# A decoder block with expert retrieval: 576 instead of 640 tokens on the dense path, its down product transposed, and one gathered tile's dot products moved into the front

## The chip, the cores and the metric

One core of a Trainium2 chip runs the whole block in one launch. The metric is the device time of one execution in microseconds (us). Engines: TensorE (PE, its weight loads PEld), VectorE (DVE), ScalarE (ACT), GpSimd (POOL), SyncE (SP, which issues most DMAs); 16 DMA engines move the data.

## The reference, cut to what matters

1024 tokens of 1024 channels. The mixing sub-layer (norm, one input projection, a gated convolution beside sliding-window attention, an output projection) is followed by expert retrieval: per token 8 heads, two key halves, the best 16 of 128 each, the best 16 sums; so 128 of 16384 experts, each with a row u and a row v.

```python
def peer_ffn(h, wq, keys, u_tab, v_tab):
    def chunk(ht):
        q = (ht @ wq).reshape(t, PEER_HEADS, 2, PEER_DK)
        sa = jnp.einsum('thd,hnd->thn', q[:, :, 0], keys[0])
        sb = jnp.einsum('thd,hnd->thn', q[:, :, 1], keys[1])
        va, ia = lax.top_k(sa, PEER_TOPK)
        vb, ib = lax.top_k(sb, PEER_TOPK)
        ...
        top, pos = lax.top_k(cand, PEER_TOPK)
        eidx = jnp.take_along_axis(cidx, pos, axis=-1)
        g = jax.nn.softmax(top, axis=-1)
        u = u_tab[eidx]
        v = v_tab[eidx]
        a = jax.nn.gelu(jnp.einsum('thkd,td->thk', u, ht))
        return jnp.einsum('thk,thkd->td', g * a, v)
```

The result is multiplied by a gate of the conditioning and added to the residual.

## The kernel before

The front works on three groups of tokens, 384, 384 and 256, with channels on the partitions (`front`, L307). A group runs 18 input projections, convolution and attention, 8 output projections, the second norm, then 16 query projections (`proj`, L235), each 24 matmuls with the group's tokens as columns; every weight is split into a high part (ScalarE, L243) and a remainder (GpSimd, L244), and high x high, high x low and low x high are summed. `keys` and `top16` find the best keys on VectorE. The rest of the selection, `finish_topk` (L540, `select` L565), is a background task that runs beside the next group: `bg(us)` (L202) is called between projections and gives each task credit at its rate, one step per unit.

The expert sum is made in two ways. Tokens 0 to 639 go the dense way: `spread` (L655) turns a token's 128 picks into a 128 x 128 matrix of coefficients, from one-hot columns `oi` (made on ScalarE, GpSimd and VectorE by the pattern HOT, L673 to L679) and partners `oj` (L683), multiplied on TensorE (L686), four tokens a step, and stores it in `gd`. The dense stage (`dense`, L750) then runs over all 128 first key indices j, each with 128 experts: `up` (L779) multiplies a row of u with h2 for all dense tokens, `weigh1` and `weigh2` (L803, L811) apply gelu and the coefficients and split the result, and `down` (L835) multiplies with v once per four j, the weights stationary and 512 channels of v moving, for 5 token blocks and 2 channel halves; `flush` (L855) adds the product to an accumulator on VectorE. All splits of u, v and the weights are threefold products as above.

Tokens 640 to 1023 go the gathered way, three tiles of 128 tokens (`gather`, L691): for each of 128 picks one indirect DMA issued from GpSimd (L713) fetches a row of u (4 KB) for each of 128 tokens into a ring of six slots, and VectorE makes a dot product (L732, the tokens' h2 copied to PSUM); then the same for v, added up in PSUM (L740). So 768 gathers of 512 KB in 774 units, all spread over the dense stage at RATE 0.49 units per credited us (`bg` in L775 and L838).

The order on an engine is laid down at build time from the program's order and readiness: fetches of the first gathered tile stand among the third group's weight splits at 953 us.

## Time and profile before

| | us |
|---|---|
| median of 3 runs | 2877.46 |
| lowest and highest | 2875.39, 2883.49 |
| span of the profiled execution | 2871.6 |
| its own time around the span | not given by the page |
| first group, front | 0 to about 360 |
| second group | about 360 to 740 |
| third group | about 740 to 1045 |
| last selections and first ups | 1045 to 1160 |
| dense and gathered stage | 1160 to 2872 |

Busy times are sums over instructions of one engine; the span is from the first to the last instruction. An idle time stands ahead of the instruction that ended it, with what released it. DMA share is the mean busy share of the 16 DMA engines; with two queues on one engine it can pass 1.

### The profile page before, as it was taken

How to read it: one execution, taken by the hardware profiler on the slowest of the kernel's cores; microseconds unless marked ns; L12 is line 12 of the kernel's file. 1: busy time of each engine (PE TensorE's matmuls, PEld its weight loads, DVE VectorE, ACT ScalarE, POOL GpSimd, SP SyncE). 2: the span in 40 equal slices, each digit the busy share in tenths (PEclk: the TensorE clock that was granted, in tenths of full speed). 3: DMA queues.
4: the chain of work that ended last, by engine and by line, in shares of the span. 5: the costliest groups of instructions: out<-in, count | busy, mean ns of one | idle time of the engine just before them, and what ended most of it. 6: DMA issues, size and time to landing. Idle time of an engine off the chain costs nothing.

```text
span 2871.6 us, 44952 instructions
## 1 busy us (share of the span) xinstructions
PE 2710.1 (94%) x15567; PEld 2441.8 (85%) x15567; DVE 2391.0 (83%) x4853; ACT 1095.5 (38%) x2193; POOL 1727.9 (60%) x1491
## 2 busy tenths in 40 slices
PE   5999989899888889999999999999999999999998
PEld 3888978788687779889999898999999889989997
DVE  5665899878799778888888898888988888888886
ACT  2455467775476633322222232222223222222221
POOL 3534476665676745666666666666666666656661
PEclk7999989999899989999999999999999999999999
DMA  6647423355334576999999999999999999999995
GB/s 224 230 145 232 123 85 129 139 199 181 99 145 138 203 234 202 347 333 348 331 320 346 348 348 333 348 323 334 337 349 323 324 349 333 331 331 342 331 334 185
DMA packets 345032, 763.69 MB, mean 266 GB/s; under 512 B 31418, under 2 KB 130138, under 8 KB 341860
## 3 DMA queue, kind: packets, MB, share of 16 engines
q0 software_dynamic: 112320, 408.99, 39.2%
q1 hardware_dynamic: 231044, 349.21, 36.4%
q8 instruction: 122, 2.00, 0.3%
q10 hardware_dynamic: 1440, 2.62, 0.2%
q14 instruction: 106, 0.87, 0.1%
HBM read 701.45 MB, written 59.24 MB: 265 GB/s over the span
## 4 chain that ended last, share of the span: by engine, by line
PE 44%; DMA 8%; DVE 6%; issue 4%; POOL 2%; ACT 1%; SPq 0%; DVEq 0%; POOLq 0%; ACTq 0%
PE pv L845 23%; PE pa L788 21%; DMA vraw<-in_v 4%; DMA uraw<-in_uT 2%; DVE pq L740 1%; DVE vdL L832 1%; DVE rows L732 1%; DMA wraw<-in_wq 1%; DVE wdL L815 1%; DVE dacc L864 1%; ACT vdH L831 1%; POOL rows L713 1%; DVE more L732 1%; POOL uL L772 0%; DVE gw L807 0%
## 5 line engine op out<-in xcount | busy, mean ns | idle before, releaser
L788 PE MATMUL pa<-h,uH 128*128 128x320 f32 x4096 | 772.0, 310 | 14.5 <-ACT uH L771 6.3
L788 PEld LDWEIGHTS pa<-h,uH 128*128 128x128 f32 x4096 | 648.2, 189 | 22.0 <-ACT uH L771 7.3
L244 POOL TENSOR_TENSOR wL<-wraw,wH 128x512 fp32r<-128x512 f32 x252 | 360.7, 1440 | 263.2 <-ACT wH L243 224.8
L845 PE MATMUL pv<-vdH,wdH 128*128 128x512 f32 x1275 | 500.2, 392 | 14.7 <-DVE dacc L864 14.5
L845 PE MATMUL pv<-vdL,wdH 128*128 128x512 f32 x1275 | 498.1, 391 | 0.1
L845 PE MATMUL pv<-vdH,wdL 128*128 128x512 f32 x1275 | 497.1, 390 | 0.0
L788 PE MATMUL pa<-h,uL 128*128 128x320 f32 x2048 | 468.9, 310 | 2.9 <-POOL uL L772 2.9
L772 POOL TENSOR_TENSOR uL<-uraw,uH 128x512 fp32r<-128x512 f32 x256 | 343.6, 1343 | 149.5 <-ACT uH L771 140.3
L713 POOL DMA_INDIRECT rows<-in_u,eidx x257 | 259.1, 1008 | 164.7 <-DVE aw L732 100.0
L713 POOL DMA_INDIRECT rows<-in_v,eidx x254 | 252.5, 994 | 160.9 <-DVE pq L740 115.6
L788 PEld LDWEIGHTS pa<-h,uL 128*128 128x128 f32 x2048 | 344.0, 189 | 3.8 <-POOL uL L772 3.8
L740 DVE SCALAR_TENSOR_TENSOR pq<-rows,aw,pq 128x1024 f32<-128x1024 f32 x253 | 324.7, 1284 | 5.0 <-DMA rows<-in_v,eidx 2.5
L864 DVE TENSOR_TENSOR dacc<-dacc,pv 128x512 f32<-128x512 f32 x310 | 212.2, 685 | 137.5 <-PE pv L845 136.7
L831 ACT CAST vdH<-vraw 128x512 fp32r<-128x512 f32 x255 | 152.7, 619 | 437.1 <-DMA vraw<-in_v 386.2
L732 DVE CUSTOM_DVE_ANT_0 rows<-rows,pq 128x1024 f32<-128x1024 f32 x257 | 307.8, 1214 | 10.5 <-DMA rows<-in_u,eidx 10.1
L771 ACT CAST uH<-uraw 128x512 fp32r<-128x512 f32 x256 | 158.4, 620 | 384.1 <-DMA uraw<-in_uT 374.1
L845 PEld LDWEIGHTS pv<-vdH,wdH 128*128 128x128 f32 x1275 | 240.0, 188 | 70.9 <-DVE dacc L864 23.1
L845 PEld LDWEIGHTS pv<-vdH,wdL 128*128 128x128 f32 x1275 | 240.0, 188 | 50.6
L845 PEld LDWEIGHTS pv<-vdL,wdH 128*128 128x128 f32 x1275 | 240.1, 188 | 47.6 <-DVE vdL L832 0.5
L678 POOL TENSOR_SCALAR oi<-iota,tr 128x128 f32<-128x128 f32 x160 | 198.5, 1242 | 109.8 <-PE gps L686 89.4
L832 DVE TENSOR_TENSOR vdL<-vraw,vdH 128x512 fp32r<-128x512 f32 x255 | 193.7, 776 | 74.1 <-ACT vdH L831 73.6
L814 ACT CAST wdH<-gw 128x640 fp32r<-128x640 f32 x128 | 93.1, 728 | 402.6 <-DVE gw L807 393.7
(251 smaller groups left out, 5118.7 us busy)
## 6 DMA issues: line engine op xcount, KB each, us to landing
uraw<-in_uT SPq DMA_DIRECT2D x256, 256.0 KB, 6.3
vraw<-in_v SPq DMA_DIRECT2D x255, 256.0 KB, 6.0
gd<-stage SPq DMA_DIRECT2D x20, 2048.0 KB, 7.5
gt<-gd SPq DMA_DIRECT2D x160, 256.0 KB, 10.2
wraw<-in_w_in SPq DMA_DIRECT2D x108, 256.0 KB, 2.8
wraw<-in_wq SPq DMA_DIRECT2D x96, 256.0 KB, 2.8
wt<-in_w_ada SPq DMA_DIRECT2D x40, 512.0 KB, 4.7
wraw<-in_w_out SPq DMA_DIRECT2D x48, 256.0 KB, 2.7
```

The lines of the kernel that those rows point to most:

```text
L244: G.tensor_tensor(wL, w, wH.bitcast(F32), op=ALU.subtract)
L678: (G if who == "P" else V).tensor_scalar(oi, iota, tr[:, 0, t:t + 1], tr[:, 2, t:t + 1], op0=ALU.is_equal, op1=ALU.mult)
L713: G.indirect_dma_start(out=r, out_offset=None, in_=table, in_offset=bass.IndirectOffsetOnAxis(ap=eidx[:, ti, k:k + 1], axis=0))
L732: V.tensor_tensor_reduce(out=r, in0=r, in1=h2, op0=ALU.mult, op1=ALU.add, scale=1.0, scalar=0.0, accum_out=aw[:, k:k + 1])
L740: V.scalar_tensor_tensor(acc, r, aw[:, k:k + 1], acc, op0=ALU.mult, op1=ALU.add)
L771: A.copy(uH, raw)
L772: G.tensor_tensor(uL, raw, uH.bitcast(F32), op=ALU.subtract)
L788: PE.matmul(AT[j][:, s, 0:n], l[:, c, :], h2[r][4 * h + c][:, s * n:s * n + n], start=(h == 0 and c == 0 and k == 0), stop=(h == 1 and c = ...
L831: A.copy(vH, raw)
L832: V.tensor_tensor(vL, raw, vH.bitcast(F32), op=ALU.subtract)
L845: PE.matmul(pt, l[:, P * tt:P * tt + P], r, start=(m == 0), stop=(m == 3 * J - 1))
L864: V.tensor_tensor(dst, dst, pt, op=ALU.add)
```

## The change

The dense tokens become 128 to 703, 576 of them, and the gathered ones 0 to 127, 704 to 767 and 768 to 1023: four tiles of 128, 64, 128 and 128 tokens. The tile of 64 lies twice on the partitions, each copy with 64 of the 128 picks, so it takes 64 fetches of u and 64 of v: 896 gathers in all. The plan of the gathered work is a list GPLAN; its first 129 units (the held h2 rows and the 128 dot products of the first tile) run as a background task in the second and third group at 0.5 units per credited us, on three slots of a new ring of four rows that lives through both stages, with h2 held in the fourth; what isn't done is drained before the dense stage. The other 779 units run in the dense stage at 0.50 on eight slots. In the dense stage both products take 288 tokens as columns (two halves): in `down` a 128 x 128 piece of v is stationary and the weights move, so the output is transposed and goes to a second output `outT`, and the gate becomes a scalar per partition, one VectorE instruction for two. A row of u comes as one DMA of 512 KB (pieces of 4 KB) for two of 256. Three PSUM buffers of one bank for `up` and three for `down`, in place of two of two banks and two. HOT gives ScalarE 3 of 8 columns, GpSimd 2, VectorE 3. The residual's rows go to memory in row form only for gathered blocks, else as they lie. Front buffers are trimmed (`oi` 6 to 4, `tr` 2 to 1, `va`, `iu` 5 to 4, `sc` 4 to 3, x 4 to 3, the two norm buffers, a selection tile halved).

```diff
-DT0, DT = 0, 640
-G0 = 640
-GT = 3
+DT0, DT = 128, 576
+HN = DT // 2
+GTILES = [(0, 128), (704, 64), (768, 128), (896, 128)]
+GOFF = np.concatenate([[0], np.cumsum([w for _, w in GTILES])]).tolist()
+GT = len(GTILES)
+NG = GOFF[-1]
+OUTS = {"out": (NG, D), "outT": (P, NC, DT)}
 J = 4
 TB = 32
-HOT = "APVV"
-RATE0, RATE = 0.0, 0.49
+HOT = "APVAVAPV"
+RATEA, RATE = 0.5, 0.5
 ORDER = True
 BACK = 0
 ADA_RATE, ADA0 = 0.3, 0.0
@@ -61,8 +65,13 @@
 FIRST, SECOND = 8, 10
 CY, ROWS, EARLY = 0, 1, 0
 TM = 384
+GPLAN = []
+for _gi, (_, _w) in enumerate(GTILES):
+    GPLAN += [("h", _gi, 0)] + [("u", _gi, k) for k in range(_w)]
+    GPLAN += [("v", _gi, k) for k in range(_w)] + [("g", _gi, 0), ("x", _gi, 0)]
+NA = 129
 RING = 6
-XB = 4
+XB = 3
...
+    rowring = gat.tile([P, 4, D], F32, name="ring")
...
-                nc.sync.dma_start(dst[r0 + P * b:r0 + P * b + P, 512 * h:512 * h + 512], xt)
-
-        for b in range(nb):
-            to_rows(x2d, t0, b, [x2T], ident)
+                nc.sync.dma_start(dst[r0:r0 + P - skip, 512 * h:512 * h + 512], xt[skip:P, :])
+
+        dcols, dat = slice(d0 - t0, d1 - t0), slice(d0 - DT0, d1 - DT0)
+        for b, gi in gblocks.items():
+            g0, w = GTILES[gi]
+            to_rows(x2d, GOFF[gi], P - w, b, [x2T], ident)
+        if d1 > d0:
+            for h in range(2):
+                nc.sync.dma_start(x2t[:, 4 * h:4 * h + 4, dat], x2T[h][:, :, dcols])
         if ROWS:
             modulate2()
-        for b in range(nb):
-            if b >= nd:
-                to_rows(h2d, t0 - G0, b, [h2H, h2L], identr)
-        if nd:
+        for b, gi in gblocks.items():
+            to_rows(h2d, GOFF[gi], P - GTILES[gi][1], b, [h2H, h2L], identr)
+        if d1 > d0:
             for k in range(2):
-                for c in range(NC):
-                    src = ch(h2[k], c)[:, 0:P * nd].bitcast(F32)
-                    at = slice(t0 - DT0, t0 - DT0 + P * nd)
-                    nc.sync.dma_start(h2s[k, :, c, at], src)
+                for h in range(2):
+                    nc.sync.dma_start(h2s[k, :, 4 * h:4 * h + 4, dat], h2[k][h][:, :, dcols].bitcast(F32))
...
-        va = [lv.tile([P, 2 * PH, 16], F32, name="va", bufs=5) for b in range(nb)]
-        iu = [lv.tile([P, 2 * PH, 16], U32, name="iu", bufs=5) for b in range(nb)]
+        va = [lv.tile([P, 2 * PH, 16], F32, name="va", bufs=4) for b in range(nb)]
+        iu = [lv.tile([P, 2 * PH, 16], U32, name="iu", bufs=4) for b in range(nb)]
...
-            for b in (range(nb) if ORDER else [*range(nd, nb), *range(nd)]):
+            for s0, b in blocks:
                 r = yield from select(va[b], iu[b])
-                if b < nd:
-                    yield from spread(t0 // P + b, *r)
-                else:
-                    place((t0 - G0) // P + b, *r)
-                    placed.append(b)
-                    if len(placed) == 1:
-                        gtask.append(add(gather(), RATE0))
+                lo, hi = max(s0, DT0), min(s0 + P, DT0 + DT)
+                if hi > lo:
+                    yield from spread(s0, lo - s0, hi - s0, *r)
+                if b in gblocks:
+                    place(gblocks[b], *r)
+                    placed.append(gblocks[b])
...
+            r3, s3 = [t.rearrange("p (h k) -> p h k", h=PH) for t in (r, src)]
+            for h0 in range(0, PH, 4):
+                hs = slice(h0, h0 + 4)
+                hot1 = sel.tile([P, 4, 16, 16], BF16, name="hot1")
+                V.tensor_tensor(hot1, s3[:, hs].unsqueeze(2).to_broadcast([P, 4, 16, 16]),
+                                rank.unsqueeze(1).to_broadcast([P, 4, 16, 16]), op=ALU.is_equal)
+                V.tensor_tensor(hot1, hot1, id4[:, hs, s, :].unsqueeze(3).to_broadcast([P, 4, 16, 16]), op=ALU.mult)
+                m = 8
+                while m > 1:
+                    V.tensor_tensor(hot1[:, :, 0:m, :], hot1[:, :, 0:m, :], hot1[:, :, m:2 * m, :], op=ALU.add)
+                    m //= 2
+                V.tensor_tensor(r3[:, hs], hot1[:, :, 0, :], hot1[:, :, 1, :], op=ALU.add)
+                yield
...
-        for q in range(P // TB):
+        for q in range(p0 // TB, p1 // TB):
...
-                    oi = gb.tile([P, P], F32, name="oi", bufs=6)
+                    oi = gb.tile([P, P], F32, name="oi", bufs=4)
...
+    def gather(plan, slots, held=None):
+
         state = {"n": 0}
-        rows = gat.tile([P, 4, D], F32, name="rows", tag="stage"), gat.tile([P, RING - 4, D], F32, name="more")
 
         def row():
-            n = state["n"] % RING
+            n = state["n"] % len(slots)
             state["n"] += 1
-            return rows[n // 4][:, n % 4, :]
-
-        def fetch(u):
-            ti, n = divmod(u, 2 * P + 2)
+            return slots[n]
+
+        def rows_of(r, src, gi, whole=True):
+            w = GTILES[gi][1]
+            part = src[GOFF[gi]:GOFF[gi] + w, :]
+            G.dma_start(r[P - w:P, :], part)
+            if w < P and whole:
+                G.dma_start(r[0:w, :], part)
+
+        def fetch(unit):
+            kind, gi, k = unit
             r = row()
-            if n == 2 * P:
+            if kind == "h":
+                rows_of(r, h2d, gi)
+            elif kind == "g":
                 G.dma_start(r, g2d)
-            elif n > 2 * P:
-                G.dma_start(r, x2d[G0 + P * ti:G0 + P * ti + P, :])
+            elif kind == "x":
+                rows_of(r, x2d, gi, whole=False)
             else:
-                if n == 0:
-                    state["hr"] = row()
...
+        ring, at = [], 0
+        for kind, gi, k in plan:
+            while gi not in placed:
                 yield
-            ti, n = divmod(u, 2 * P + 2)
-            if n == 0:
-                aw = state["aw"]
-                h2 = state["hr"]
-                if "pq" in env:
-                    h2 = env["pq"].tile([P, D], F32, name="pq")
-                    A.copy(h2, state["hr"])
+            while at < len(plan) and len(ring) < len(slots) - 1 and plan[at][1] in placed:
+                ring.append(fetch(plan[at]))
+                at += 1
             r = ring.pop(0)
-            k = n % P
-            if n < P:
+            w = GTILES[gi][1]
+            if kind == "h":
+                h2 = held if held is not None else env["pq"].tile([P, D], F32, name="pq")
+                A.copy(h2, r)
+                aws[gi] = gat.tile([P, P], F32, name="aw", bufs=2)
+            elif kind == "u":
                 V.tensor_tensor_reduce(out=r, in0=r, in1=h2, op0=ALU.mult, op1=ALU.add, scale=1.0,
-                                       scalar=0.0, accum_out=aw[:, k:k + 1])
-            elif n == P:
+                                       scalar=0.0, accum_out=aws[gi][:, k:k + 1])
...
-        pa = es.enter_context(tc.tile_pool(name="pa", bufs=2, space=PSUM, side="right", reuse_waits="tile"))
+        pa = es.enter_context(tc.tile_pool(name="pa", bufs=3, space=PSUM, side="right", reuse_waits="tile"))
...
-                    raw = da.tile([P, 4, P], F32, name="uraw", bufs=2)
-                    nc.sync.dma_start(raw, a["uT"][j, :, 4 * h:4 * h + 4, :])
+                    if h == 0:
+                        both = da.tile([P, NC, P], F32, name="uraw", bufs=2)
+                        nc.sync.dma_start(both, a["uT"][j])
+                    raw = both[:, 4 * h:4 * h + 4, :]
...
+        def up(j):
+            for s in range(2):
+                AT[j, s] = pa.tile([P, 512], F32, name="pa")
+                for h in range(2):
+                    uH, uL = U[j][h]
+                    for c in range(4):
                         for k, (l, r) in enumerate(((uH, 0), (uH, 1), (uL, 0))):
...
+                            PE.matmul(AT[j, s][:, 0:n], l[:, c, :], h2[r][4 * h + c][:, s * n:s * n + n],
+                                      start=(h == 0 and c == 0 and k == 0), stop=(h == 1 and c == 3 and k == 2))
+            U.pop(j)
...
-            pt = AT.pop(j)[:, :, 0:n]
-            A.activation(pt, pt, AF.Gelu_apprx_tanh)
             gw = GW[j] = gws[j % 2]
-            V.tensor_tensor(gw.rearrange("p (s b t) -> p s b t", s=2, t=TB), pt.rearrange("p s (b t) -> p s b t", t=TB),
-                            GG[j // J][:, :, (j % J) * TB:(j % J) * TB + TB].rearrange("p (s b) t -> p s b t", s=2),
-                            op=ALU.mult)
+            for s in range(2):
+                pt = AT.pop((j, s))[:, 0:n]
+                A.activation(pt, pt, AF.Gelu_apprx_tanh)
+                V.tensor_tensor(gw[:, s * n:s * n + n].rearrange("p (b t) -> p b t", t=TB),
+                                pt.rearrange("p (b t) -> p b t", t=TB),
+                                GG[j // J][:, s * n // TB:(s + 1) * n // TB, (j % J) * TB:(j % J) * TB + TB],
+                                op=ALU.mult)
...
-            for tt in range(nt):
-                bg(2.57)
-                next(extra, None)
-                pt = pv.tile([P, 512], F32, name="pv")
-                m = 0
-                for j in js:
-                    vH, vL = VV[j, dh]
-                    for l, r in ((W[j][0], vH), (W[j][0], vL), (W[j][1], vH)):
-                        PE.matmul(pt, l[:, P * tt:P * tt + P], r, start=(m == 0), stop=(m == 3 * J - 1))
-                        m += 1
-                adds.append((g, tt, dh, pt))
-                if len(adds) > LAG:
-                    flush()
+            for x in range(4):
+                for s in range(2):
+                    bg(1.6)
+                    next(extra, None)
+                    pt = pv.tile([P, 512], F32, name="pv")
+                    m = 0
+                    for j in js:
+                        vH, vL = VV[j, dh]
+                        for l, r in ((vH, W[j][0]), (vH, W[j][1]), (vL, W[j][0])):
+                            PE.matmul(pt[:, 0:n], l[:, P * x:P * x + P], r[:, s * n:s * n + n],
+                                      start=(m == 0), stop=(m == 3 * J - 1))
+                            m += 1
+                    adds.append((g, 4 * dh + x, s, pt[:, 0:n]))
+                    if len(adds) > LAG:
+                        flush()
...
-            if g == P // J - 1:
-                r0 = DT0 + P * tt
-                V.tensor_tensor(dst, dst, fin["g2"][dh], op=ALU.mult)
-                V.tensor_tensor(dst, dst, fin["x2"][tt, dh], op=ALU.add)
-                A.dma_start(out[r0:r0 + P, ds], dst)
-
-        fin["x2"], fin["g2"] = {}, {}
+            if g == last:
+                V.scalar_tensor_tensor(dst, dst, mod[:, 40 + dc:41 + dc], fin[dc][:, s * n:s * n + n],
+                                       op0=ALU.mult, op1=ALU.add)
+                A.dma_start(outT[:, dc, s * n:s * n + n], dst)
...
-        for t in gtask:
-            t[1], t[2] = RATE, GC0
+        rows = gat.tile([P, 4, D], F32, name="rows", tag="stage")
+        slots = [rows[:, x, :] for x in range(4)] + [rowring[:, x, :] for x in range(4)]
+        add(gather(GPLAN[NA:], slots), RATE, GC0)
...
-        pv = es.enter_context(tc.tile_pool(name="pv", bufs=2, space=PSUM))
+        pv = es.enter_context(tc.tile_pool(name="pv", bufs=3, space=PSUM))
...
+        if not gtask:
+            gtask.append(add(gather(GPLAN[:NA], [rowring[:, x, :] for x in range(3)], rowring[:, 3, :]), RATEA))
...
+    drain(gtask[0])
```

## Rows read from the trace of the kernel before

**Rows 1.** The page's busy time, and its chain that ended last.

```profile
PE 2710.1 (94%) x15567; PEld 2441.8 (85%) x15567; DVE 2391.0 (83%) x4853; ACT 1095.5 (38%) x2193; POOL 1727.9 (60%) x1491
...
PE 44%; DMA 8%; DVE 6%; issue 4%; POOL 2%; ACT 1%; SPq 0%; DVEq 0%; POOLq 0%; ACTq 0%
PE pv L845 23%; PE pa L788 21%; DMA vraw<-in_v 4%; DMA uraw<-in_uT 2%; DVE pq L740 1%; DVE vdL L832 1%; DVE rows L732 1%; DMA wraw<-in_wq 1%; DVE wdL L815 1%; DVE dacc L864 1%; ACT vdH L831 1%; POOL rows L713 1%; DVE more L732 1%; POOL uL L772 0%; DVE gw L807 0%
```

**Rows 2.** Stages: busy us of PE, PEld, DVE, ACT, POOL; clock, DMA share, GB/s.

```profile
360.00:740.00 380.00, 347.72 (x2156) 313.21 (x2157) 321.89 (x1025) 253.83 (x599) 240.48 (x186) 0.97 0.41 145
740.00:1045.00 305.00, 259.11 (x1814) 230.56 (x1812) 249.38 (x871) 193.63 (x457) 208.83 (x159) 0.92 0.44 153
...
1160.00:2820.00 1660.00, 1649.20 (x9259) 1502.02 (x9260) 1446.78 (x1880) 444.43 (x721) 1064.40 (x987) 1.00 0.96 336
```

**Rows 3.** Who waited for whom after 1160 us: us in total, times, longest.

```profile
DVE dacc L864 <- PE pv L845: 124.2, 156, 2.9
...
PE pv L845 <- DVE dacc L864: 14.5, 14, 4.5
```

**Rows 4.** Timeline of PE in the dense stage: start, us, line, tiles, shape, count.

```profile
2000.67 0.75 PE L788 MATMUL pa<-h,uH 128*128 128x320 f32 x4
...
2001.55 0.75 PE L788 MATMUL pa<-h,uH 128*128 128x320 f32 x4
...
2006.05 0.39 PE L845 MATMUL pv<-vdH,wdH 128*128 128x512 f32 x1
...
2008.77 0.39 PE L845 MATMUL pv<-vdH,wdH 128*128 128x512 f32 x1
```

**Rows 5.** Timeline of PE in the third group's query projections; fourteen matmuls apart.

```profile
1023.42 0.28 PE L247 MATMUL pj<-h2L,wH 128*128 128x256 f32 x1
...
1025.09 0.28 PE L247 MATMUL pj<-h2H,wH 128*128 128x256 f32 x1
```

**Rows 6.** DMA queues from 1160 to 2820 us: packets, MB, share of 16 engines.

```profile
q0 software_dynamic: 108000, 393.26, 65.0%
q1 hardware_dynamic: 145163, 162.92, 30.1%
```

**Rows 7.** Short stretches of the dense stage, columns as in rows 2.

```profile
1515.00:1520.00 5.00, 5.00 (x34) 4.83 (x32) 4.80 (x6) 2.25 (x4) 2.59 (x3) 1.00 1.04 407
...
1555.00:1560.00 5.00, 5.00 (x31) 4.58 (x30) 4.57 (x5) 1.88 (x4) 4.52 (x4) 1.00 0.74 251
1700.00:1750.00 50.00, 50.00 (x290) 46.21 (x289) 44.89 (x71) 12.92 (x22) 34.34 (x31) 1.00 0.99 354
```

**Rows 8.** VectorE lines: min/median/max ns, then groups: busy us, mean ns.

```profile
L732 DVE CUSTOM_DVE_ANT_0 rows<-rows,pq x257: 1196/1214/1222, 1050.2 to 2531.6; 128x1024 f32<-128x1024 f32 x129
...
L815 DVE TENSOR_TENSOR wdL<-gw,wdH x128: 810/821/2444, 1078.1 to 2832.3; 128x640 fp32r<-128x640 f32 x128
...
L161 DVE SCALAR_TENSOR_TENSOR acc<-wt,cond,acc x31: 1237/1285/2311, 23.9 to 220.3; 128x1024 f32<-128x1024 f32 x31
...
L815 DVE TENSOR_TENSOR wdL<-gw,wdH 128x640 fp32r<-128x640 f32 x119 | 123.2, 1035 | 3.8 <-ACT wdH L814 3.8
...
L161 DVE SCALAR_TENSOR_TENSOR acc<-wt,cond,acc 128x1024 f32<-128x1024 f32 x31 | 47.5, 1532 | 6.7 <-DMA wt<-in_w_ada 6.4
```

**Rows 9.** Groups from 360 to 1045 us: count, busy us, mean ns, idle before.

```profile
L678 DVE TENSOR_SCALAR oi<-iota,tr 128x128 f32<-128x128 f32 x320 | 129.7, 443 | 24.4 <-PE gps L686 22.4
L683 DVE TENSOR_TENSOR oj<-iota,tr 128x512 f32<-128x512 f32 x160 | 118.9, 764 | 8.2 <-PE gps L686 4.2 <-ACT tr L662 3.2
...
L678 POOL TENSOR_SCALAR oi<-iota,tr 128x128 f32<-128x128 f32 x160 | 198.5, 1242 | 109.8 <-PE gps L686 89.4 <-ACT tr L662 13.8 <-DVE iu L557 1.9
...
L713 POOL DMA_INDIRECT rows<-in_u,eidx x3 | 2.9, 972 | 0.8 <-issue 0.6
...
L686 PE MATMUL gps<-oj,oi 128*128 128x128 f32 x1280 | 197.1, 295 | 38.2 <-DVE oi L678 16.6 <-DVE oj L683 7.4 <-POOL oi L678 5.5
```

**Rows 10.** PE's waits in the third group, 740 to 1045 us.

```profile
PE pj L247 <- POOL wL L244: 13.1, 10, 5.4
```

**Rows 11.** The gather line from 900 to 1160 us.

```profile
DMA to landing us min/median/max: 4.1/6.1/8.7
```

160 lines of the change are left out of this document (70 added, 90 removed).

## The prediction

> **What bounds the kernel now.** I read the chain that ended last, busy time by stage, then the stage that holds most of the time and its DMA. TensorE is busy 2710.1 of 2871.6 us, and the chain is 44% matmul, its two largest lines the two products of the dense stage [rows 1]. By stage [rows 2]: in the second and third token groups (360 to 740 and 740 to 1045 us) TensorE is at 91% and 85%, VectorE at 85% and 82%, so neither alone is the bound; from 1160 to 2820 TensorE works 1649.2 of 1660 us at a granted clock of 1.00 and sets the pace. VectorE has 13% idle there, most of it (124.2 us) waiting for the product it evicts; TensorE waited 14.5 us for evictions [rows 3]. The DMA engines carry a share of 0.96. So three resources stand at 99, 87 and 96%: whoever shortens the first meets the other two.
>
> **Part 1: the dense products on TensorE.** Matmuls are pipelined, so I take start to start, not busy time. Six of 320 columns take 0.88 us, 147 ns each; twelve of 512 take 2.72 us, 227 ns each [rows 4]. Fourteen of 256 in the front take 1.67 us, 119 ns each, every one with a new stationary tile [rows 5]. The three lie on a line, 0.42 ns a column and some 12 ns besides; weight loading shows no floor down to 256. So 288 columns cost 132 ns (an estimate from these rows).
> Before, one expert row j takes 48 matmuls of 320 (up) and 30 of 512 (down): 48 x 0.147 + 30 x 0.227 = 13.85 us, 128 of them 1773 us. After, up is 48 of 288, and down, with v stationary, 8 chunks x 2 halves x 3 = 48 of 288: 96 x 0.132 = 12.67 us, 1622 in all. TensorE alone would give back 151 us.
>
> **Part 2: what DMA and VectorE allow in that stage.** The stretch from 1160 to 2820 holds 1660/13.85 = 119.9 rows j. Its gather queue took 65.0% of the 16 engines and moved 393.26 MB, 750 gathers: 1.439 us of all engines for one. The other queue took 30.1%, 4.17 us per j [rows 6]. The gathers of the dense stage stay 768 (the 128 added ones go to the front), but their pace rises from 0.49 to 0.50 per credited us, 6.4 per j: 9.21 us. The loads of u and v stay, the dense coefficients shrink by a tenth (1.376 to 1.343 MB per j): 4.07. The u rows become pieces of 4 KB: at the gather's price that saves 0.15, at the present one nothing. In all 13.1 to 13.3, taken 13.25 us of DMA beside 12.67 us of TensorE, a share of 1.05. Can the engines do that? Stretches of 5 us reach 1.04 at 407 GB/s, with dips to 0.74 between; the best 50 us hold 0.99 at 354 [rows 7]. At 0.99 a row j takes 13.38 us, at the peaks 12.67. I take 13.0, half way: the ring of eight slots and two whole u buffers fill some of the dips.
> VectorE has 1446.8/119.9 = 12.07 us per j. More gather units per j add 0.12 x 1.21 = 0.15; the evictions stay (16 of 288 columns for 10 of 512 per four j: a tenth fewer columns, six more starts), the split of the weights shrinks by a tenth of its 1.04 us [rows 8]. So 12.1 of 13.0 us, 93%: no bound, but TensorE's 14.5 us of waiting for evictions may grow; the half way value holds it.
> The gathers last for 779 units less some 18 in the tail, 761/6.4 = 119 j. Sum: 119 x 13.0 + 9 x 12.67 = 1661 for 1773: **-112 us**, between -151 and -67.
>
> **Part 3: the front, second and third group.** Added: 129 units of one tile, 128 of them dot products, from the time the first block's experts are placed, on a ring of three slots. Removed: the columns for 64 tokens.
> The dots stand on VectorE among the front's own work. In the dense stage one takes 1.214 us, minimum and maximum 1.196 and 1.222, with one input in PSUM; in the front both inputs lie in SBUF. Instructions with two SBUF inputs have another spread: the split of the weights a median of 821 and a mean of 1035 ns (maximum 2444), and the nearest in size, the 128x1024 accumulation of the modulation, 1285 and 1532 [rows 8]. So a dot costs between 1.21 and 1.26 x 1.21 = 1.53 us; I take the nearest row's factor, 1532/1285 = 1.19: 1.45 us, 129 of them 187 us.
> The Trainium skill has a rule that speaks against this move (GPSIMD Engine Reference, Specifications): GpSimd's SBUF interface is shared with VectorE, and contended when a VectorE instruction has two SBUF inputs. By it the dots go to the upper price, by the PSUM row they stay at 1.21; the sum below would move by +10 or by -32 us. The spread in rows 8 agrees with the rule.
> Removed on VectorE: 160 groups of four tokens become 144, and the pattern gives VectorE 3 of 8 columns for 1 of 2: of 129.7 + 118.9 us, 320 columns become 216 and 160 partner tiles 144, 88 + 107 us [rows 9]. That is 54 us of instruction time, some 46 of busy time, in which neighbours overlap. The selection in two halves adds about 8. Net +149 us on VectorE, in two groups where it is busy 321.9 + 249.4 = 571 of 685 us [rows 2]: 720. Filled to 98% that takes 735 us: **+50 us**, and VectorE paces the front in place of TensorE. The others have room: TensorE loses 16 groups of columns and 32 transposes; GpSimd gets 129 issues of 0.97 us and loses 16 columns of 1.24: 449 + 105 = 554 of 735 [rows 2, 9]; ScalarE takes the columns VectorE gives away.
> New waits: a fetch waits on GpSimd's queue for the dot that frees its slot, and behind it stand the weight splits and columns that TensorE needs (it already waited 13.1 us for splits in the third group [rows 10]). A slot turns round in 0.97 (issue) + 6.1 (median landing [rows 11]) + 1.45 = 8.5 us, three slots give a dot every 2.8 us, and 735 us for 129 ask for one every 5.7. So I take nothing, and 0 to +30 into the range; nothing below zero, since no wait goes away with it. Four column buffers for six and fewer score and x buffers: TensorE stood 38.2 us before the column products [rows 9]; from nothing to that much again, taken as nothing since VectorE paces.
> Costed at nothing: fewer and larger stores and loads on SyncE's queue, beside engines that are 41 and 44% busy with DMA in these groups [rows 2] (without that cover, the weights' loads behind them would be late); the copy of the held rows on ScalarE; the last evictions with two VectorE instructions for three.
>
> **Sum.** Against the profiled execution: 2871.6 - 112 + 50 = 2809.6 us of span. What lies around its span the page doesn't give; the median of the runs is 5.9 us above the span, so 2815 us.
>
> **Rivals.**
> *TensorE stays the bound.* The dips of rows 7 fill, DMA runs at its peaks, a dot costs 1.21. Dense at 12.75 us per j, 1632 (-141); front 571 - 46 + 8 + 156 = 689 us of VectorE for 685: +4. 2871.6 - 141 + 4 + 5.9 = 2740. For it: 407 GB/s was reached; against: no 50 us above 0.99. Chance 0.20.
> *The DMA engines hold where they are* (the slower end). If their mean can't rise above 0.96, a row j takes 13.25/0.96 = 13.8 us whatever TensorE does: the dense stage gains 119 x 0.05 + 9 x 1.18 = 17, the front still pays 50: 2910. It decides from 13.5 us per j upward, where the dense gain falls below the front's 50. For it: 96% now; against: the dips, which are lack of demand. Chance 0.12.
> *The dots don't run ahead*, so that the change doesn't do what it says. If the third group's 43 fall behind its other work, they are drained before the dense stage at the ring's 2.8 us with TensorE idle (the granted clock of that group is 0.92 already): 120 us for the 62 counted, +60: 2875. Chance 0.08.
> *A ceiling on memory traffic.* A row j will move 6.4 x 0.524 + 1.343 = 4.70 MB, 371 GB/s at 12.67 us. If the best 50 us (354) are a ceiling, it takes 13.28 us; dense -78, 2849. Against it: 407 GB/s. Chance 0.06. The Trainium skill (DMA: Bandwidth & Descriptors, Specifications) puts one core's share of HBM at about 358 GB/s; as a ceiling that would give an estimate of 2830, and the 407 differs from it.
>
> **How the numbers follow.** The forecast has 0.54; by its bounds it reaches from about 2775 to 2860, and 2815 is the time. The range 2740 to 2875 leaves out the slower rival, half of the first one's spread and half of the third's. A difference under 0.3% (8.6 us) can't be told from no change. Faster than that: 0.50 of the forecast and 0.20, 0.06, 0.02 of rivals, 0.78; within: 0.08; slower: 0.14.
>
> **What the profile after would show.** Matmuls of 288 columns 132 ns apart; through the dense stage a DMA share near 1.0, VectorE above 90%, and TensorE a few per cent idle, waiting for evictions or for u and v; the third group ending near 1095 instead of 1045, VectorE above 95% in both groups; dots at 1.3 to 1.5 us in the front, 1.2 behind it. The prediction is wrong if TensorE waits tens of us for weight splits in the front, if dots bunch at the end of the third group, or if the dense row j is far from 13.0 us.

## The result and the profile after

The changed kernel takes 3109.4 us (3103.2 to 3113.2), the kernel before 2876.7: a ratio of 1.0805, 95% interval 1.0785 to 1.0824. It is slower by 8%, where 2815 and a gain were forecast, and lies outside the range.

The page after, as rows 1 of before: busy time, then the chain that ended last by engine.

```profile
PE 2694.7 (87%) x17743; PEld 2533.3 (81%) x17743; DVE 2553.6 (82%) x5339; ACT 1112.6 (36%) x2420; POOL 1832.0 (59%) x1609
...
DVE 37%; PE 32%; DMA 12%; issue 12%; POOL 4%; ACT 3%; SPq 0%; another core or an unknown queue 0%; DVEq 0%; POOLq 0%; ACTq 0%
```

TensorE's work has hardly changed [rows 1], but its part of the chain fell from 44% to 32% and VectorE's rose from 6% to 37%. Where the time went is read by stage: first group, second, third, start of the dense stage, its long stretch, end (columns as in rows 2).

```profile
0.00:350.30 350.30, 301.50 (x1570) 262.90 (x1571) 222.40 (x627) 149.72 (x321) 154.75 (x114) 0.91 0.58 191
350.30:849.80 499.50, 381.28 (x1950) 325.96 (x1948) 418.23 (x1218) 244.27 (x577) 321.96 (x255) 0.84 0.60 199
849.80:1255.80 406.00, 308.66 (x1937) 271.27 (x1937) 332.20 (x1022) 244.81 (x591) 252.18 (x208) 0.86 0.51 174
1255.80:1368.30 112.50, 92.14 (x617) 88.83 (x618) 101.63 (x279) 35.94 (x79) 44.46 (x39) 0.91 0.61 196
1368.30:3047.30 1679.00, 1554.93 (x11269) 1528.99 (x11268) 1445.10 (x2134) 427.54 (x836) 1055.52 (x991) 0.98 0.94 331
3047.30:3111.40 64.10, 56.17 (x408) 55.37 (x406) 34.09 (x64) 10.27 (x20) 3.10 (x3) 0.96 0.34 112
```

The same cut of before:

```profile
0.00:345.20 345.20, 301.85 (x1554) 260.52 (x1555) 222.30 (x626) 149.92 (x322) 155.63 (x113) 0.92 0.58 195
345.20:739.70 394.50, 358.31 (x2217) 323.48 (x2216) 336.32 (x1122) 261.14 (x615) 245.45 (x189) 0.97 0.41 143
739.70:1045.50 305.80, 259.41 (x1817) 230.86 (x1815) 250.18 (x875) 194.41 (x458) 209.31 (x161) 0.92 0.44 153
```

Below, "the front" is the time from the second group's first copy of k to the first product of up, and "a row j" is the time from the first to the last product of up divided by 127. The front went from 700.3 to 905.5 us (+205.2), the 127 rows from 1771.9 to 1807.0 (13.95 to 14.23 us each, +35.1); the first group gives +5.1, the end -5.6. Together +239.8, the whole difference of the spans (3111.4 for 2871.6). So the front cost four times the 50 us it was costed at, and the dense stage gave back nothing.

The term the dense gain rested on is as forecast: 36 products of 288 columns between these two lines take 4.76 us, 132 ns each.

```profile
2000.10 0.29 PE L817 MATMUL pa<-h,uL 128*128 128x288 f32 x1
...
2004.86 0.29 PE L817 MATMUL pa<-h,uL 128*128 128x288 f32 x1
```

### The profile page after: what moved, and what is told of

The parts are those of the page before. It is cut to its first block, busy times and chain, and to the rows that moved or that the text cites. A ratio compares the mean times of both kernels' runs of the same rounds, so it can differ in the third digit from the quotient of the medians.

```text
span 3111.4 us, 49852 instructions
## 1 busy us (share of the span) xinstructions
PE 2694.7 (87%) x17743; PEld 2533.3 (81%) x17743; DVE 2553.6 (82%) x5339; ACT 1112.6 (36%) x2420; POOL 1832.0 (59%) x1609
## 4 chain that ended last, share of the span: by engine, by line
DVE 37%; PE 32%; DMA 12%; issue 12%; POOL 4%; ACT 3%; SPq 0%; another core or an unknown queue 0%; DVEq 0%; POOLq 0%; ACTq 0%
PE pv L876 10%; DMA vraw<-in_v 8%; DVE pq L768 8%; PE pj L257 7%; PE pa L817 6%; DVE ring L759 4%; DVE vdL L862 4%; PE gps L710 3%; DVE dacc L895 2%; DVE rows L759 2%; DMA ring<-in_u,eidx 2%; DVE gw L836 2%; POOL oi L702 2%; POOL wL L254 1%; DVE hot L650 1%
## 5 line engine op out<-in xcount | busy, mean ns | idle before, releaser
L817 PE MATMUL pa<-h,uH 128*128 128x288 f32 x4096 | 848.1, 302 | 102.1 <-DVE gw L836 91.5
L876 PE MATMUL pv<-wdH,vdH 128*128 128x288 f32 x2040 | 612.2, 300 | 48.7 <-DVE dacc L895 40.6
L817 PE MATMUL pa<-h,uL 128*128 128x288 f32 x2048 | 613.2, 300 | 2.8 <-POOL uL L803 2.7
L876 PE MATMUL pv<-wdH,vdL 128*128 128x288 f32 x2040 | 609.9, 299 | 0.4 <-DVE vdL L862 0.4
L876 PE MATMUL pv<-wdL,vdH 128*128 128x288 f32 x2040 | 608.6, 298 | 0.0
L741 POOL DMA_INDIRECT ring<-in_u,eidx x288 | 318.8, 1107 | 204.7 <-DVE aw L759 85.1
L876 PEld LDWEIGHTS pv<-wdH,vdH 128*128 128x128 f32 x2040 | 390.7, 192 | 56.4 <-DVE dacc L895 46.4
L876 PEld LDWEIGHTS pv<-wdH,vdL 128*128 128x128 f32 x2040 | 390.4, 191 | 1.1 <-DVE vdL L862 1.1
L876 PEld LDWEIGHTS pv<-wdL,vdH 128*128 128x128 f32 x2040 | 390.6, 191 | 0.1
L768 DVE SCALAR_TENSOR_TENSOR pq<-ring,aw,pq 128x1024 f32<-128x1024 f32 x223 | 285.6, 1281 | 1.1
```

What stands on the lines that cost most here:

```text
L741: G.indirect_dma_start(out=r, out_offset=None, in_=a[kind], in_offset=bass.IndirectOffsetOnAxis(ap=eidx[:, gi, k:k + 1], axis=0))
L768: V.scalar_tensor_tensor(acc, r, aw[:, k:k + 1], acc, op0=ALU.mult, op1=ALU.add)
L817: PE.matmul(AT[j, s][:, 0:n], l[:, c, :], h2[r][4 * h + c][:, s * n:s * n + n], start=(h == 0 and c == 0 and k == 0), stop=(h == 1 and c = ...
L876: PE.matmul(pt[:, 0:n], l[:, P * x:P * x + P], r[:, s * n:s * n + n], start=(m == 0), stop=(m == 3 * J - 1))
```

## The experiments

Each is an edit of the changed kernel. Totals are of one execution each (of two for a_late); beside them the kernel before took 2877 to 2882 us. Eight of these kernels have in essence the same front (changed, a_nogather, a_gdma, a_gdve, a_pa4, a_pqsb, a_gwfirst, a_ring6), and it took 889.5 to 905.5 us in them; seven have the same dense stage (changed, a_noearly, a_dots, a_traffic, a_fetch, a_2slots, a_apart), with a row j of 14.09 to 14.23 us. Smaller differences than these 16 us and 0.14 us tell nothing. The changed kernel has the longest row of the seven, so its 127 rows lose between 18 and 35 us. In a_split0 and a_back all 908 units run at the pace of 0.50 and go on behind the last row, so their totals say nothing of the front.

| kernel | front, us | row j, us | total, us |
|---|---|---|---|
| before | 700.3 | 13.95 | 2877 |
| changed | 905.5 | 14.23 | 3109 |
| a_noearly: no early units | 766.5 | 14.14 | 2964 |
| a_dots: early dots, no fetches | 824.6 | 14.10 | 3034 |
| a_traffic: fetches nobody reads | 829.3 | 14.09 | 3025 |
| a_fetch: fetches, tiny dots | 867.3 | 14.16 | 3066 |
| a_2slots: ring of two | 920.9 | 14.22 | 3128 |
| a_apart: fetches and dots unconnected | 925.1 | 14.18 | 3148 |
| a_buffers: no early units, old buffers | 732.6 | 14.14 | 2923 |
| a_pattern: a_buffers, old pattern | 691.4 | 14.18 | 2890 |
| a_split0: no early units, tokens 0 to 575 dense | 749.8 | 13.94 | 3070 |
| a_back: a_pattern with that split | 693.2 | 14.07 | 3024 |
| a_nogather: dense stage almost without gather units | 903.0 | 12.82 | 2930 |
| a_gdma: its fetches, tiny dots and sums | 905.3 | 13.22 | 2989 |
| a_gdve: its dots and sums, no fetches | 899.3 | 13.41 | 3010 |
| a_pa4: PSUM buffers 4 and 2 for 3 and 3 | 904.0 | 14.51 | 3152 |
| a_pqsb: sums in SBUF, PSUM buffers 4 and 4 | 889.5 | 14.94 | 3189 |
| a_gwfirst: weighting ahead of the units | 900.3 | 14.54 | 3152 |
| a_ring6: six dense slots for eight | 898.8 | 14.45 | 3137 |
| a_late: a_back at pace 0.58 | 693.4 | 15.15 | 3017 |

### The early units in the front

**No early units.**

```
-            gtask.append(add(gather(GPLAN[:NA], [rowring[:, x, :] for x in range(3)], rowring[:, 3, :]), RATEA))
+            gtask.append(None)
+            aws[0] = gat.tile([P, P], F32, name="aw", bufs=2)
+            V.memset(aws[0], 0.5)
```

> The changed kernel without the 129 early units: no row is fetched and no dot product made in the front (the activations of those 128 experts are a constant, so the gathered tile's output is not the real one); every buffer stays as trimmed. Marks: the first matmul of up came at 1045.5 us before and at 1255.8 after. Theory A (the dots' work on VectorE, with the same busy share as before): VectorE's work in the second and third group falls from 756 to about 609 us, at 83% that is 734 us, up begins near 1080. Theory B (the trimmed buffers): up still begins after 1150. Theory C (the fetches and waits in the queues): near 1040, below what the work alone would say. The dense stage should keep its 14.2 us per row j in all of them.

Up began at 1117.4, between the marks of theories A and B: the units cost 139 us of the front, and 66 are left without them. So there are two causes.

**Fetches with tiny dots, dots without fetches, fetches that nobody reads.**

```
+                m = D if held is None else 32                  # a_fetch: dot over r[:, 0:m]
...
-            else:                                              # a_dots
+            elif held is None or k < 2:
...
+                if held is None:                               # a_traffic: no dot in the front
                     V.tensor_tensor_reduce(out=r, in0=r, in1=h2, op0=ALU.mult, op1=ALU.add, scale=1.0,
```

> The early rows are fetched and waited for as in the changed kernel, but the dot product covers 32 of 1024 columns (so it is not the real one). Theory A (work on VectorE): most of the delay goes, up begins near 1090. Theory C (VectorE and GpSimd standing in order behind landings and behind each other): the waits stay, up begins after 1170. Theory B (buffers): as without early units.

> The early dot products are made in full, but on rows that already lie there: only the first two fetches are issued, GpSimd does not wait for slots and VectorE for no landing (the dots are not the real ones). Theory A (work): up begins near 1240, within 20 us of the changed kernel's 1255.8. Theory C (fetches and waits): most of the delay goes, up begins before 1130.

> The early rows are fetched into the three slots, each fetch waiting only for the fetch before it in its slot, and nobody reads them: no dot product, no wait of VectorE (the activations of those 128 experts are a constant, so the gathered tile's output is not the real one). The front takes 767 us without early units, 867 with fetches and tiny dots that wait for them. Theory C (VectorE in order behind landings): at most 25 us more than without, 792 or less. Rival I (GpSimd's issues, its waits and the traffic): 830 or more.

Dots alone cost 58 us in the front (75 by the first up, since 18 of the 128 ran in the first group). Fetches alone cost 63, with nobody reading them; with tiny dots that wait for the rows 101, of which the tiny dots' own work on VectorE may be a part (it is busy 609 us in a_fetch, 582 in a_traffic); everything together 139. None of theories A, C and I holds alone: dots, fetches and waiting cost 58, 63 and 38 us, more than the 139 they cost together.

VectorE's busy share is not fixed in this stage. Without early units, then with the dots alone (columns as in rows 2):

```profile
350.90:1117.40 766.50, 639.12 (x3888) 562.88 (x3886) 559.97 (x1983) 484.30 (x1165) 398.93 (x334) 0.90 0.39 134
```

```profile
367.40:1192.00 824.60, 654.02 (x3877) 571.66 (x3876) 710.00 (x2203) 485.46 (x1167) 442.64 (x336) 0.88 0.36 126
```

That is 73% and 86%, for 84% before (586.5 of 700.3 us) and 83% in the changed kernel (750.4 of 905.5). The 110 dots in that stretch brought 150 us of work and 58 us of time: 92 us of the work went into idle time.

GpSimd's part: the mean issue in the changed kernel is 1.245 us where 0.972 was read [rows 9], and behind it stand the weight splits and columns TensorE needs. TensorE's waits of these two kinds in the changed kernel, in the second group, then in the third:

```profile
PE gps L710 <- POOL oi L702: 16.3, 18, 2.5
...
PE pj L257 <- POOL wL L254: 9.1, 12, 1.4
...
PE gps L710 <- POOL oi L702: 18.3, 18, 3.7
PE pj L257 <- POOL wL L254: 17.3, 22, 2.2
```

That is 61 us, for 20 before; without early units it is 34, with unread fetches 65. VectorE's part, in a_fetch from 350 to 1217 us, and what follows for the path, that kernel's chain from 350 to 850 us:

```profile
DVE ring L760 <- DMA ring<-in_u,eidx: 115.4, 55, 7.8
```

```profile
by line: DMA ring<-in_u,eidx 28.7%; issue 8.0%; PE gps L710 7.6%; PE pj L257 6.5%; DMA x<-in_xT 3.5%; POOL oi L702 2.9%; DVE hot L653 2.8%; POOL wL L254 2.7%; DVE oi L702 2.7%; DVE oj L707 2.4%; DVE ring L760 2.1%; DVE hot L650 2.0%; PE po 
```

VectorE works in order. When the row of the next dot has not landed, everything of the front that is queued behind it stands too. In the changed kernel it stood 33.0 us so:

```profile
DVE ring L759 <- DMA ring<-in_u,eidx: 33.0, 21, 5.6
```

**Two slots; fetches and dots unconnected.**

```
-... [rowring[:, x, :] for x in range(3)], rowring[:, 3, :]
+... [rowring[:, x, :] for x in range(2)], rowring[:, 3, :]     # a_2slots
...
+            r = row() if held is None or k < 2 else slots[2]   # a_apart: fetch into slot 2
+            if held is not None and kind == "u":
+                r = slots[k % 2]                               #          dot on slots 0 and 1
```

> Early units on a ring of two slots instead of three, one row ahead of the dot instead of two. Theory C (the loop of slot, issue and landing is on the path): the front, 906 us, grows by 60 us or more, VectorE waits over 100 us for landings. By the prediction's working (8.5 us a round, so a dot every 4.2 us where one every 5.7 us is asked for) nothing changes: within 15 us.

> In the front all 128 early rows are fetched and all 128 dot products made in full, but the fetches go to a third slot that nobody reads and the dots take rows that lie there (an addition with a maximum for the product with a sum, not the real ones): no fetch waits for a dot, no dot for a landing. The front from the second group's first product to the first matmul of up took 906 us in the changed kernel, 767 without early units, 825 with dots alone and 867 with fetches and tiny dots. Theory C (the loop of slot, issue and landing between two queues in order): about 825 to 845. Rival I (GpSimd's issues and the memory traffic themselves): 880 or more.

A slot fewer cost 15 us, less than theory C asked, at the edge of what the prediction's working allows and not clear of the spread of equal fronts; VectorE stood 58 us behind landings. a_apart does not tell what it was made for: with one slot to write into, each fetch waited for the one before it.

```profile
POOL ring L741 <- DMA ring<-in_u,eidx: 175.7, 72, 6.7
```

It shows something else. VectorE waits for no row in it, and the front is as slow as ever (925 us), TensorE standing 62.2 and 54.5 us behind GpSimd's splits and columns: waits at the head of GpSimd's queue can cost this front as much as those at the head of VectorE's.

### The 66 us without early units

```
+ name="oi", bufs=6; "tr" 2; XB = 4; "sc" 4; "va", "iu" 5; tmp("sq"); "rstd" 2           # a_buffers
+ halves = rowring[:, 1:3, :].rearrange("p a (c q) -> p a c q", c=4); ring of 3 rows
+ HOT = "APVV"                                                     # a_pattern: this as well
+ DT0, DT = 0, 576; GTILES = [(576, 64), (640, 128), ...]; NA = 0  # a_split0 (alone), a_back (with both)
```

> The changed kernel without the early units (as in the run without them, where the second group took 398 us and the third 369, for 394 and 306 before), and with the front buffers of before: six column buffers, two for the transposed experts, four for x, four for scores, five for the top values, the squares and the norm factors on their own again; the attention's scores lie in ring rows that are free without early units, and the dense ring has seven slots. Theory B (the trimmed buffers cost the 66 us that are left in the front): the third group falls to 330 us or less. Theory F (the change moved column work into the third group, 80 groups of four tokens there for 64 before, and 64 in the second for 96): the third group stays within 15 us of 369.

> The changed kernel without early units, with tokens 0 to 575 dense and 576 to 1023 gathered: the same 144 groups of four tokens, but 96 of them in the second group and 48 in the third; the trimmed buffers stay. Theory F (columns moved into the third group): the third group falls by 32 groups' worth, from 369 to about 310 us, and the second rises from 398 by less than that. Theory B (buffers): the third group stays above 345 us.

> No early units, the front buffers of before, tokens 0 to 575 dense (96 groups of four columns in the second token group, 48 in the third) and the column pattern of before; what is left of the change in the front is 16 groups of columns fewer, the selection in two halves and the stores for the transposed output. The front took 700 us before, 767 with trimmed buffers and the new split, 733 with the buffers of before, 750 with the first split. If buffers, split and pattern are the whole of the 66 us: 685 to 710 us. If something else of the change costs there: 720 or more. The gathers that the dense stage does not finish run on behind it, as in the run with the first split.

> The run with the front buffers of before and without early units (front 733 us), now with the column pattern of before: half of the columns on VectorE, a quarter each on ScalarE and GpSimd, for three, two and three of eight. If the pattern costs: the front falls by 15 us or more, to 718 or less. If the split of the tokens costs: within 8 us of 733.

The old buffers give back 34 us (766.5 to 732.6), but not where theory B put them: the third group fell only from 369 to 356, the second from 398 to 376. In a_split0 theory F's shift came (435 and 315 us for 398 and 369), but the sum moved by 17 us alone. The column pattern gives back 41 us (732.6 to 691.4), the larger piece, and with it the split no longer matters (693.2). The pattern was tried on the old buffers alone, so how the two share their 75 us in the other order is open. What is left, 691.4 for 700.3, is too small to read.

Both pieces show on VectorE where it waits for TensorE to free a column buffer. In the front of a_noearly, a_buffers and a_pattern, then of before:

```profile
DVE oi L702 <- PE gps L710: 94.8, 100, 7.7
```

```profile
DVE oi L702 <- PE gps L710: 47.6, 53, 5.0
```

```profile
DVE oi L702 <- PE gps L710: 24.9, 28, 3.1
```

```profile
DVE oi L678 <- PE gps L686: 22.4, 32, 2.9
```

The pattern moved 72 of 576 columns from VectorE to ScalarE. With the new pattern (a_buffers, from 350 to 1040 us) a column on ScalarE is two instructions, 398 and 485 ns, on VectorE one of 414:

```profile
L700 ACT ACTIVATE oi<-oi,tr,ng 128x128 f32<-128x128 f32 x211 | 95.5, 485 | 0.2
L702 DVE TENSOR_SCALAR oi<-iota,tr 128x128 f32<-128x128 f32 x211 | 85.3, 414 | 49.4 <-PE gps L710 47.5 <-ACT stage L711 0.3
L699 ACT ACTIVATE oi<-iota,ng 128x128 f32<-128x128 f32 x212 | 81.8, 398 | 35.2 <-PE gps L710 27.7 <-POOL oi L702 6.1
```

So 72 x 0.41 = 30 us of instructions were taken from VectorE and 72 x 0.88 = 64 us put on ScalarE, which also makes the high parts of the weights and empties PSUM for TensorE, in order; in busy time of the front VectorE lost 29 us (584.3 to 555.7) and ScalarE gained 45 (434.0 to 478.6). That this is the way by which the 41 us arise is argued from these lines. TensorE's own waits for ScalarE's columns grew by little (4.3 to 7.2 us, its weight loads' from 7.2 to 16.7), so the way stays open; the 41 us are measured.

### The dense stage

**Without gather units, with their DMA alone, with their VectorE work alone.**

```
-        add(gather(GPLAN[NA:], slots), RATE, GC0)                          # a_nogather
+        few = [(k, gi, 0) for gi in range(GT) for k in "hvgx" if gi or k != "h"]
+        add(gather(few, slots), RATE, GC0)
...
+                m = 32 if held is None else D                              # a_gdma: dots, sums on [:, 0:m]
...
-            else:                                                          # a_gdve
+            elif held is not None or (kind, gi) == ("v", 0) and k < 9:
```

> The changed kernel with its early units, but only 15 of the 779 units of the dense stage (nearly all fetches, dot products and sums over gathered rows of that stage are left out, so the gathered tokens' output is not the real one). The dense products, weightings, splits and evictions stay as they are. Theory G (the products of 288 columns can't be kept up with three and three PSUM buffers whatever else VectorE does): the row j stays above 13.3 us. Theory E (the gathers' work on VectorE and on the DMA engines holds the stage): the row j falls to 12.7 to 12.9 us, TensorE is busy to 99% and its waits for VectorE under 30 us.

> The changed kernel; in the dense stage all 779 units are fetched, but the dot products and the sums cover 32 of 1024 columns (so the gathered tokens' output is not the real one). Without nearly all of these units the row j took 12.7 us, with them 14.2. Theory H (the DMA engines hold the stage): the row j stays between 13.7 and 14.2 us at a DMA share near 0.95, VectorE under 50%. Theory E (VectorE's work and its queue hold it): the row j falls to 13.2 us or less, and the DMA share rises over 1.0.

> The reverse: in the dense stage only the first nine rows are fetched, and every dot product and sum is made in full on rows that lie there (an addition with a maximum stands for the product with a sum, so the output is not the real one); VectorE does the same number of instructions of the same size. Theory H (DMA): the row j falls to 12.7 to 13.0 us. Theory E (VectorE): it stays above 13.7 us.

Without the units TensorE never stops: theory G falls, three and three PSUM buffers are enough for 12.82 us a row. With DMA alone a row takes 13.22, with VectorE alone 13.41, with both 14.23. Alone they cost 0.40 and 0.59 us a row, together 1.41, which is 0.42 more than the two added. Neither H nor E holds alone. From 1400 to 2900 us, first a_gdma, then a_gdve, then the changed kernel:

```profile
1400.00:2900.00 1500.00, 1465.78 (x10944) 1453.48 (x10943) 732.28 (x2075) 415.20 (x804) 1030.90 (x965) 1.00 0.98 360
```

```profile
1400.00:2900.00 1500.00, 1444.93 (x10757) 1428.92 (x10756) 1379.13 (x2045) 402.63 (x793) 332.39 (x239) 1.00 0.34 105
```

```profile
1400.00:2900.00 1500.00, 1396.34 (x10143) 1374.30 (x10142) 1288.72 (x1946) 380.90 (x745) 949.12 (x892) 0.98 0.94 333
```

When VectorE is at hand to free slots, the DMA engines carry 0.98 and 360 GB/s through 1500 us. When rows lie ready, VectorE is busy to 92%. Together both fall, to 0.94 and 86%, as they would if each waits for the other. The chain through the long stretch, in order of before, the changed kernel and a_gdma, says where:

```profile
by line: PE pv L845 37.9%; PE pa L788 34.5%; DMA vraw<-in_v 7.3%; issue 4.7%; DMA uraw<-in_uT 2.2%; DVE pq L740 2.2%; DVE vdL L832 2.1%; DVE rows L732 1.8%; DVE wdL L815 1.0%; DVE more L732 0.9%; ACT vdH L831 0.9%; DVE dacc L864 0.9%; DVE g
```

```profile
by line: PE pv L876 16.4%; issue 15.5%; DMA vraw<-in_v 14.1%; DVE pq L768 13.3%; PE pa L817 10.8%; DVE vdL L862 6.7%; DVE ring L759 4.7%; DVE rows L759 4.3%; DVE dacc L895 4.3%; DVE gw L836 2.9%; DVE wdL L845 1.5%; ACT vdH L861 1.4%; DMA ur
```

```profile
by line: PE pv L878 37.3%; PE pa L819 35.5%; DMA vraw<-in_v 6.3%; issue 5.4%; DMA uraw<-in_uT 4.1%; DMA ring<-in_v,eidx 1.5%; DMA ring<-in_u,eidx 1.4%; DVE vdL L864 1.3%; DMA rows<-in_u,eidx 1.2%; DVE dacc L897 1.1%; POOL rows L741 0.9%; PO
```

The two products are 72% of it before, 73% with the DMA alone, 27% in the changed kernel. In their place stand VectorE's sums, the loads of v and 15.5% of issue, time in which the engine waited for nothing that the profile shows. One stretch of that chain:

```profile
2001.79 1.71 DVE vdL L862
2003.52 5.54 DMA vraw<-in_v
2009.08 0.63 ACT vdH L861
2009.73 0.70 DVE vdL L862
2010.45 2.86 DMA vraw<-in_v
...
2017.06 1.57 DVE vdL L862
2018.64 5.30 DMA vraw<-in_v
2023.94 0.91 issue
2024.85 0.63 ACT vdH L861
2025.50 0.69 DVE vdL L862
```

A half row of v has two raw buffers. The next load starts when VectorE has made the low part of the one before, whose place in VectorE's queue is behind the gather units; it lands 2.9 to 5.5 us later, among the gathers' traffic; then VectorE stands for it (2.92 us here), its gather units and evictions queued behind. By this reading busy VectorE makes the loads late, busy DMA makes them long, and late loads stop VectorE. It fits the excess of both over the sum, but it is not shown. VectorE's waits for the high part of v from 1400 to 2800 us, in order of before, the changed kernel, a_gdma and a_gdve:

```profile
DVE vdL L832 <- ACT vdH L831: 51.7, 37, 3.4
```

```profile
DVE vdL L862 <- ACT vdH L861: 54.7, 28, 4.7
```

```profile
DVE vdL L864 <- ACT vdH L863: 87.5, 60, 4.4
```

```profile
DVE vdL L862 <- ACT vdH L861: 11.8, 12, 1.6
```

The wait comes with the gathers' traffic: of the four it is short only in a_gdve. But it was as long before, when TensorE still set the pace, and longest in a_gdma, where VectorE had time for it. In the same stretch TensorE's products waited 88.3 us for VectorE's weighting and evictions in the changed kernel, 9.0 before. A third raw buffer for v would test the loop and was not tried.

**Buffers, order and slots.**

```
- pa bufs=3, pv bufs=3
+ pa bufs=4, pv bufs=2                                        # a_pa4
+ pa bufs=4, pv bufs=4, h2 and acc in rowring[:, 3, :]        # a_pqsb
...
-                if not ahead:                                # a_gwfirst
-                    bg(3.2)
                 if (mid, post)[h]:
                     (mid, post)[h]()
+                if not ahead:
+                    bg(3.2)
...
- slots = [rows[:, x, :] for x in range(4)] + [rowring[:, x, :] for x in range(4)]
+ slots = [rows[:, x, :] for x in range(4)] + [rowring[:, x, :] for x in range(2)]   # a_ring6
```

> Four one-bank buffers for the product of up instead of three, two for that of down instead of three; all else as in the changed kernel. In 1400 to 3060 us TensorE and its weight loads stood 167 us behind the weighting of VectorE and 74 us behind evictions. Theory D (the products of up are released in lockstep): the first falls under 40 us, the row j goes from 14.2 to 13.5 us or less, the total falls by 60 us or more. Rival E (VectorE and the DMA engines set the pace, the wait only shows it): the waiting moves to the evictions, the row j stays within 0.2 us of 14.2, the total within 25 us.

> The sum over gathered rows in SBUF instead of PSUM, and the two banks that it leaves given to the dense products: four buffers for up and four for down, for three and three; seven ring slots for eight. Two buffers for down instead of three took the row j from 14.2 to 14.6 us. Theory D (too few buffers between TensorE and VectorE): TensorE's waits for VectorE in the dense stage, 240 us, fall under 120 and the row j comes to 13.6 us or less. Rival E (VectorE's work sets the pace): the waits stay, or VectorE's own work grows as its second input moves to SBUF, and the row j is 14.0 us or more.

> In the dense stage the weighting of a row j and the split of the weights are put ahead of the gather units of that half instead of behind them; nothing else changes. Theory J (the weighting, which frees the bank that TensorE's next product of up needs, stands in VectorE's queue behind up to two gather units of 1.2 us that wait for their rows): TensorE's waits for it fall from 150 us to under 60, the row j from 14.2 to 13.8 us or less, the total by 50 us. Rival K (VectorE is late as a whole): the waiting moves to the evictions, the row j within 0.1 us.

> Six slots for gathered rows in the dense stage instead of eight (as many as before), all else as in the changed kernel. Theory L (fetches and sums hold each other up through the slots): the row j grows from 14.2 to 14.5 us or more and the DMA share falls under 0.92. Rival: the row j stays within 0.1 us of 14.2, the ring is deep enough with six.

The forecasts of theory D failed twice, that of theory J too; a_pqsb is no clean test of D, since VectorE's sums grew with it (below). In each the wait for the weighting shrank and one for evictions took its place, larger; a_gwfirst from 1400 to 2800 us:

```profile
PEld pv L876 <- DVE dacc L895: 109.1, 48, 5.2
PE pv L876 <- DVE dacc L895: 97.3, 42, 5.0
PEld pa L817 <- DVE gw L836: 26.3, 23, 2.7
PE pa L817 <- DVE gw L836: 20.6, 18, 2.5
```

For 28.1, 24.2, 79.0 and 64.1 in the changed kernel. The waiting moved to the evictions, as rivals E and K said, but the rows grew by 0.28 us in a_pa4 and 0.32 in a_gwfirst where those asked for at most 0.2 and 0.1. That VectorE is late as a whole there, so that whichever of its products is put first another comes late, fits this and is not shown. Six slots cost 0.22 us a row at a DMA share of 0.92, in between theory L and its rival: slots are a part of the coupling, not the main one.

**All units in the dense stage, a pace that ends with it.**

```
-RATEA, RATE = 0.5, 0.5
+RATEA, RATE = 0.5, 0.58                                      # on a_back
```

> No early units, the front of the run with the buffers, the split and the pattern of before (693 us), and the dense stage at 0.58 units per credited us instead of 0.50, so that the 908 units end with it. With 7.4 units a row j moves 7.4 x 1.439 + 4.07 = 14.7 us of DMA; at a share of 0.96 that is 15.3 us. By the DMA engines: j at 15.0 to 15.4, a total of 2990 to 3040, no better than the 3024 with the units behind the stage. By the marginal price of a unit (0.22 us): j near 14.5 us, a total of 2910 to 2930. Either way it is faster than the changed kernel (3109) and slower than before (2877).

A row takes 15.15 us at a share of 0.95, as by the DMA engines; the marginal price fell. The total is 3016.6 us, 1.048 of before (1.040 to 1.055): better than the changed kernel, but not than before. From the first up to the end it takes 1973.9 us, for 1855.6 in the changed kernel: having the 129 units early saves 118 us there, in kernels that differ in split, ring and pace too, and costs 139 in the front. No version tried beats the kernel before.

## Why the prediction was wrong, point by point

- *The dense products, 12.67 us a row:* right, 132 ns a product and 12.82 us a row without gather units. That they were right brought nothing, since TensorE no longer set the pace.
- *The DMA engines at 13.0 us a row:* nearly right for the DMA alone (13.22, share 0.98). The forecast's 1.02 was not reached. (At a share of 1.04 the working gives 13.25/1.04 = 12.74, not 12.67; half way is then 13.06.) On the ceiling of the fourth rival the runs speak: 360 GB/s is the mean over 1500 us of a_gdma. The 358 GB/s that the Trainium skill gives for one core's share of HBM (DMA: Bandwidth & Descriptors, Specifications) agree with that as a mean; peaks of 5 us went beyond [rows 7].
- *"So 12.1 of 13.0 us, 93%: no bound":* the step that failed in the dense stage. VectorE's work was sized well (1445.1 us in the long stretch), but a share of 93% is no cover. Its work alone holds a row at 13.41, and beside the DMA's at 14.23. The prediction costed each resource against the row, took the largest, and so left out that the resources wait for each other; which of these waits makes the 0.42 us beyond the sum stays open. The gain of 112 became a loss of 18 to 35.
- *"Filled to 98% that takes 735 us":* the step that failed in the front, and the largest. The work was nearly right (750.4 us on VectorE for 720; dots 1.426 us each for 1.45, and 1.211 in the dense stage as before, so the upper price was right). The Trainium skill's rule that VectorE instructions with two SBUF inputs contend with GpSimd for the shared interface (GPSIMD Engine Reference, Specifications) agrees with this trace: the median of these dots is 1.217 us, the longest 3.110. But VectorE did not come to pace the front: it was busy 83% of it, and 86% with the dots alone. That 83 is so near to the 84% of before is chance, since without early units it was 73%. What filled the 205 us instead: 139 for the early units, of which the dots' work alone cost 58, and 66 that have nothing to do with them, 34 for the buffers and 41 for the pattern less a remainder of 9. All but the dots were terms that the prediction put at nothing.
- *The fetches on GpSimd's queue, nothing, 0 to +30:* wrong. Unread fetches cost 63 us, waiting for rows with tiny dots another 38. The working compared a round of 8.5 us with the mean pace of the dots. But dots come in bursts, two or three a projection in the second group by the program, and what pays is not the ring but what is queued behind the wait on both engines. What was named as a sign of error came: TensorE stood 26 us for weight splits and 35 for GpSimd's columns.
- *Fewer buffers, nothing, 0 to 38.2:* 34 us, at the upper bound. The cover "VectorE paces" was not there.
- *The columns given to ScalarE, "have room":* wrong, 41 us. It was costed as work taken from VectorE alone; that it was a longer way to TensorE is argued.
- *Rivals:* "the DMA engines hold where they are" came nearest (2910, a row at 13.8), with the right sign by luck: the front's loss was four times the one in it, and the engines can carry 0.98. That the dots would bunch at the end did not come (33 of 128 ran in the third group, to 1093 us).
- *Signs:* the third group ended at 1256, not 1095; VectorE was at 83% there, not above 95%; the dense DMA share 0.94, not near 1.0.

## What to carry to other kernels

An engine that is idle a sixth of the time in a stage where all engines hand work to each other in order is not room for new work at its full size, and its present busy share does not tell the stage's new length either: here the share went from 73 to 86% when 150 us of dots came in, and the stage grew by 58 us. Leave the work in and take its transfers out, and the other way round, to see what each costs. Work that must wait for a transfer, put into the queue of an engine that others wait for, costs what stands behind it, and where several resources stand at 93 to 100% of a row, the row can be longer than the largest of them. A buffer or a column given up "since another engine sets the pace" costs its full price when that engine does not, 34 and 41 us here.
